# A hybrid layer's mixer: state-space constants whose second forms are exchanged halves, angles counted in turns, and the recurrent decay as an exponential

## The chip, the cores and the metric

The kernel runs on one core of a Trainium2 chip. The metric is the device time of one execution in microseconds. The core's engines work side by side, each through its own queue in order: PE (matrix products, with weight loads shown as PEld), DVE and POOL (element-wise work), ACT (functions from tables, evictions, scaled copies) and SP, which issues the DMAs. An instruction waits on semaphores for what it reads, and everything behind it on its engine waits with it.

## The reference

One layer over 2048 positions of width 1024: a mixer of three branches, then a mixture of experts. The change is in branches B and C of the mixer.

```python
z = rms_norm(h, norm_g) @ w_in                # split into A (gated MLP), B (recurrent), C (state space)

def mixer_rglru(x_raw, g_raw, ...):           # B: 384 channels
    xc = causal_depthwise_conv(x_raw, conv_w, conv_b)
    r = sigmoid(xc @ rg_w + rg_b)             # per head of 64
    i = sigmoid(xc @ ig_w + ig_b)
    log_a = -8.0 * r * softplus(-lam)
    a = exp(log_a)
    b = sqrt(-expm1(2.0 * log_a)) * (i * xc)
    h = linear_recurrence(a, b)               # h_t = a_t h_{t-1} + b_t
    return h * gelu(g_raw)

def mixer_s5(x_raw, a_re, a_im, log_dt, b_re, b_im, c_re, c_im, d, ...):   # C: 16 groups x 16 channels
    lam = a_re + 1j * a_im                    # 64 complex states in each group
    lam_bar = exp(lam * exp(log_dt))
    b_bar = (lam_bar - 1.0) / lam * (b_re + 1j * b_im)
    state = linear_recurrence(lam_bar, b_bar x)
    y = gelu((c_mat state).real + d * x)
    return y * sigmoid(y @ glu_w + glu_b)

y = concat(rms_norm(y_a), rms_norm(y_b), rms_norm(y_c)) @ w_out
h = h + y
h = h + hierarchical_moe(rms_norm(h))         # top-1 group, top-2 experts in it
return rms_norm(h, final_norm_g)
```

## The kernel before

The program has two parts. The first makes the three branches, the output projection and the routing; the second (from about 835 us) runs the experts block by block. Everything the change touches is in the first.

**How the first part is staged.** The sequence is done in two halves (h = 0, 1) of 1024 positions. For each half the columns of `w_in` come in chunks of 256: for h = 0 in the order A0, C, B0, B1, B2, A1, A2. A chunk is multiplied in full precision by three matmuls on split operands (lines 90 to 92, output `z`), the operands being a high part and a remainder of the transposed, normalised input (`xT`) and of the weights (`w`, made on ACT at lines 212 and 216 and on POOL). What belongs to a branch after its matmuls is written as a generator. A small class `Flow` advances all living generators by one step at each tick, and ticks stand between the matmuls of the chunks (after every twelve of a B chunk); a `yield n` lets n ticks pass, a `yield 0` goes on in the same tick after the others. A table `TURNS`, keyed by a generator's number and its step, overrides some of those numbers. So the program's order on each engine is fixed when it is built: constants, recurrent pieces and weight preparation are woven into the sequence of matmuls, and at run time each queue goes through that order.

**`s5_consts`** makes the constants of branch C once, on the fly, while the B chunks are multiplied. For the 16 groups it needs the powers 0 to 8 of `lam_bar` (`pw`: real and imaginary part, powers, groups), the input matrices `bb1` and `bb2` (real and imaginary rows stacked on 128 partitions, and a second form), the output matrices `tcc[0]` and `tcc[1]` in the same two forms, and tables of cosine and sine of 130 multiples of each state's angle. It goes through the groups four at a time, so in four rounds:

- `angles` (lines 661 to 687): the multiples `k * phi` of an angle that is split into a coarse part `phi` and a remainder `plo` are formed on 128 x 4 x 130 elements, reduced by multiples of 2 pi with a rounding through integers and a two-part constant, clamped, and given to the sine on ACT; the cosine is one minus twice the squared sine of the half angle. Both tables go to device memory (`cstT`), and their last columns to `cs128`.
- the loop at lines 700 to 738: `outer` multiplies powers by matrices on POOL and DVE (128 x 512 in `big`, 128 x 576 in `m1..`/`m2..`), sums and differences of the products are made on POOL, the input matrices are transposed on PE and evicted by ACT, and both forms go to device memory (`cstP`, five slots of 16 x 128 columns: 0 and 1 are the two forms of the input matrices, 3 and 4 those of the output matrices, 2 the direct kernel). The direct kernel `kp` of the four groups comes from a PE product and goes to `kpad`, from which eight DMAs (line 740) fill slot 2 after the last round.

The state-space work itself (`c_batch`, two groups at a time, eight batches per half) reads `cstP` and `cstT` back with DMAs (lines 784 to 788), so it starts after the fourth round.

**`b_post`** is the recurrent branch for one piece: 128 channels (i = 0..2) of 512 positions (q = 0, 1) of a half, so twelve pieces in all, six for each half. The convolution runs on DVE on the matmul's result (`bxc`), the two gate products on PE (line 922, bank `m`), tanh of the half argument on ACT in place of the sigmoids (line 923). Then the decay and its root (lines 926 to 941). With `sp` the softplus times two in column 0 of `b_cols` and `tr` the tanh of the gate, the second tanh (line 926) is T = tanh(-log_a / 2), the root of T is made on ACT, and on DVE 1/(1 + T), from which sqrt(1 - a^2)/2 = sqrt(T)/(1 + T) and a = 2/(1 + T) - 1. A scan on DVE makes the recurrence, POOL multiplies by the gate (`bgg`), ACT squares it (line 946) and PE sums the squares (line 950).

A function of ACT needs its table set: gelu and tanh are in one set here, the sine and the root in others, and a change of set is an instruction of its own (ACT_TABLE_LOAD), which the compiler places.

## Time and profile before

| | us |
|---|---|
| median of 3 runs (lowest to highest) | 1661.69 (1660.15 to 1671.78) |
| profiled execution, its own time | 1667.31 |
| its span | 1665.5 |
| PE busy in the span | 1510.0 (91%) |
| DVE busy | 1028.5 (62%) |
| ACT busy | 915.6 (55%) |
| POOL busy | 693.2 (42%) |

Busy shares are means over stages with different limits, so they say little about one edit. The page's second part cuts the span into 40 slices of 41.6 us and gives each engine's busy tenths and the granted clock of PE in them:

```profile
PE   7885689989999999989589969999999999999993
...
DVE  6399876367365165777888877578788767403001
ACT  6455345656755556543144635666566656656662
POOL 1286412142202153442144534556555555545442
PEclk8998799999999999999789989999999999999996
```

PE is near full in most slices; the third to fifth are the ones in which DVE stands at 8 or 9 and PE falls to 5 and 6. These are the slices of the constants and of the first four recurrent pieces. The time of a stage is read from the engine whose queue is full in it; the prediction cuts the span at 88 and 204 us, where the constants' rounds begin and end, and at 300 and 600.

### The profile page before, as it was taken

What the parts mean: (1) busy time and instruction counts of PE and PEld (TensorE: products, weight loads), DVE (VectorE), ACT (ScalarE), POOL (GpSimd) and SP (SyncE); (2) the same over time, 40 slices, a digit from 0 to 9 for tenths busy, and PEclk for the clock granted to TensorE, in tenths of its full rate; (3) what the DMA queues carried; (4) which work ended last, traced back from release to release, by engine and by line L of the source; (5) the groups of instructions that cost most, each with busy time, mean ns of one, the idle gap of its engine ahead of it and who ended that gap; (6) DMA issues with size and microseconds to landing.
All of it is one profiled execution on the core that took longest, in us unless ns stands there. A gap on an engine that the chain in (4) does not pass through costs nothing.

```text
span 1665.5 us, 25734 instructions
## 1 busy us (share of the span) xinstructions
PE 1510.0 (91%) x8389; PEld 1295.1 (78%) x8390; DVE 1028.5 (62%) x1813; ACT 915.6 (55%) x2029; POOL 693.2 (42%) x553
## 2 busy tenths in 40 slices
PE   7885689989999999989589969999999999999993
PEld 6763469966788999989578858888888888888882
DVE  6399876367365165777888877578788767403001
ACT  6455345656755556543144635666566656656662
POOL 1286412142202153442144534556555555545442
PEclk8998799999999999999789989999999999999996
DMA  6232572331262352940677878678978876633442
GB/s 165 70 71 60 95 208 78 114 102 51 77 209 64 134 202 77 339 155 37 220 256 228 247 239 243 172 196 261 280 228 244 251 223 195 176 83 96 86 115 79
DMA packets 210063, 267.47 MB, mean 161 GB/s; under 512 B 30600, under 2 KB 174160, under 8 KB 209936
## 3 DMA queue, kind: packets, MB, share of 16 engines
q1 hardware_dynamic: 185456, 203.52, 38.6%
q0 software_dynamic: 24480, 62.27, 15.5%
q8 instruction: 78, 1.28, 0.3%
q14 instruction: 49, 0.40, 0.1%
HBM read 217.09 MB, written 76.94 MB: 177 GB/s over the span
## 4 chain that ended last, share of the span: by engine, by line
PE 61%; DVE 14%; DMA 6%; ACT 3%; issue 2%; POOL 1%; SPq 1%; POOLq 0%; DVEq 0%; ACTq 0%
PE pg L1693 21%; PE z L90 6%; PE z L92 6%; PE z L91 6%; PE pd L1734 4%; PE pd L1733 4%; PE pd L1732 4%; DMA stg<-in_expert_w_up_dram 3%; DVE ring L1601 2%; DVE ring L1619 2%; PE pt L1700 2%; DVE btr L932 1%; PE pt L1705 1%; PE ph L1700 1%; PE m L246 1%
## 5 line engine op out<-in xcount | busy, mean ns | idle before, releaser
L1693 PE MATMUL pg<-ring,xs 128*128 x2016 | 488.2, 395 | 14.1 <-DVE ring L1619 13.0
L1693 PEld LDWEIGHTS pg<-ring,xs 128*128 128x128 f32 x2016 | 378.5, 190 | 94.3 <-issue 16.5
L90 PE MATMUL z<-w,xT 128*128 128x256 f32 (+1 forms) x848 | 252.3, 297 | 17.9 <-ACT xT L302 8.9
L169 POOL TENSOR_TENSOR w<-raw,w 128x512 fp32r<-128x512 f32 x84 | 115.0, 1371 | 348.3 <-ACT raw L216 302.9
L92 PE MATMUL z<-w,xT 128*128 128x256 f32 (+1 forms) x848 | 246.5, 291 | 5.8 <-DVE xT L169 5.7
L91 PE MATMUL z<-w,xT 128*128 128x256 f32 (+1 forms) x848 | 245.9, 290 | 0.0
L1601 DVE TENSOR_SCALAR ring<-stg,gcol 128x512 fp32r<-128x512 f32 x242 | 133.3, 612 | 166.4 <-PE pg L1693 86.7
L1619 DVE SCALAR_TENSOR_TENSOR ring<-stg,gcol,ring 128x512 fp32r<-128x512 f32 x248 | 218.4, 940 | 0.0
L90 PEld LDWEIGHTS z<-w,xT 128*128 128x128 f32 x848 | 166.1, 196 | 21.7 <-issue 10.4
L92 PEld LDWEIGHTS z<-w,xT 128*128 128x128 f32 x848 | 165.6, 195 | 7.2 <-DVE xT L169 7.2
L91 PEld LDWEIGHTS z<-w,xT 128*128 128x128 f32 x848 | 166.2, 196 | 1.7 <-issue 1.7
L1897 POOL DMA_INDIRECT hd<-yb,tab x41 | 75.8, 1848 | 180.5 <-ACT yb L1836 180.5
L1732 PE MATMUL pd<-ring,hh 128*128 x336 | 131.5, 391 | 1.7 <-DVE hh L1638 1.7
L1733 PE MATMUL pd<-ring,hh 128*128 x336 | 131.2, 390 | 0.0
L1734 PE MATMUL pd<-ring,hh 128*128 x336 | 131.2, 390 | 0.0
L1911 POOL TENSOR_TENSOR hs<-hs,hu 128x256 f32<-128x256 f32 x84 | 102.1, 1215 | 54.0 <-ACT hu L1815 51.5
L1946 POOL TENSOR_TENSOR yb<-yb,gf 128x1024 f32<-128x1024 f32 x40 | 117.0, 2924 | 6.8 <-ACT hu L1861 6.8
L171 DVE SCALAR_TENSOR_TENSOR ht<-z,rsd,ht 128x256 f32<-128x256 f32 x176 | 84.7, 483 | 49.8 <-PE z L92 40.3
L90 PE MATMUL z<-xT,w 128*128 128x512 f32 x256 | 113.4, 443 | 0.2 <-ACT xT L302 0.2
L212 ACT ACTIVATE w<-raw,vec 128x256 fp32r<-128x256 f32 x176 | 86.6, 495 | 48.1 <-PE z L92 47.2
L91 PE MATMUL z<-xT,w 128*128 128x512 f32 x256 | 103.6, 405 | 0.2 <-DVE xT L169 0.2
L92 PE MATMUL z<-xT,w 128*128 128x512 f32 x256 | 103.1, 403 | 0.0
(443 smaller groups left out, 2862.0 us busy)
## 6 DMA issues: line engine op xcount, KB each, us to landing
stg<-in_expert_w_gate_dram SPq DMA_DIRECT2D x62, 512.0 KB
stg<-in_expert_w_up_dram SPq DMA_DIRECT2D x62, 512.0 KB
stg<-in_expert_w_down_dram SPq DMA_DIRECT2D x60, 512.0 KB
raw<-in_w_in_dram SPq DMA_DIRECT2D x48, 256.0 KB
raw<-in_w_out_dram SPq DMA_DIRECT2D x24, 512.0 KB
ht<-in_x_dram SPq DMA_DIRECT2D x16, 512.0 KB
yp<-yTd SPq DMA_DIRECT2D x8, 1024.0 KB
hd<-ht SPq DMA_DIRECT2D x16, 512.0 KB
```

What stands on the lines that cost most here:

```text
L90: nc.tensor.matmul(ps, ah, bh, start=first, stop=False)
L91: nc.tensor.matmul(ps, ah, bl, start=False, stop=False)
L92: nc.tensor.matmul(ps, al, bh, start=False, stop=last)
L169: tt = lambda o, a, b, op, e=V: e.tensor_tensor(out=o, in0=a, in1=b, op=op)
L1601: x = v.tensor_scalar(out=ring[:, r, 0, sl], in0=src[:, sl], scalar1=g, scalar2=None, op0=OP.mult)
L1619: x = v.scalar_tensor_tensor(out=ring[:, r, 1, sl], in0=src[:, sl], scalar=g, in1=hi, op0=OP.mult, op1=OP.subtract)
L1693: i = t.matmul(pg[f], xx[j // 2], w[j % 2], start=k == 0 and j == 0, stop=k == 7 and j == 2)
L1732: t.matmul(pd[n], hh[:, 0, kf], w[0], start=kf == 0, stop=False)
L1733: t.matmul(pd[n], hh[:, 0, kf], w[1], start=False, stop=False)
L1734: i = t.matmul(pd[n], hh[:, 1, kf], w[0], start=False, stop=kf == 3)
L1911: g.tensor_tensor(out=o, in0=o, in1=hu[:, f * 256:(f + 1) * 256], op=OP.mult).then_inc(s_hm, 1)
L1946: g.tensor_tensor(out=z, in0=z, in1=gf, op=OP.mult).then_inc(p_z, 1)
```

## The change

Three things are changed.

**Second forms as exchanged halves.** The sign of `swp` and the place of the minus are arranged so that slot 1 of `cstP` is slot 0 with its two halves of 64 columns exchanged, and slot 4 is slot 3 with its two halves of 64 partitions exchanged. So in each round `outer` runs twice instead of four times on each of POOL and DVE, two POOL additions go, four of the eight transposes and one of two evictions go, and slots 1 and 4 are written by two DMAs each, from the same tiles as slots 0 and 3.

**Angles in turns.** `phi` and `plo` are kept in turns (one turn is 2 pi), and `trn` is the whole angle in turns. ACT makes `k * trn` with a column scale; adding and subtracting 12582912 rounds it to whole turns on DVE; eight fused DVE steps, one group of 128 x 130 at a time, make `k * phi - round` and add `k * plo`; the factor 2 pi is the scale of the sine, with the sign of the lower half folded into it (`sg2`). The square, the scale and shift that make the cosine, and the two copies into `cs128` are on ACT instead of POOL and DVE.

**The decay as an exponential.** Column 3 of the tile `b_cols` holds minus 4 times the softplus, and a = exp(log_a) comes straight from ACT, in place of the reciprocal. With T as before, sqrt(1 - a^2)/2 = (1 + a) sqrt(T)/2, which is one fused DVE step on `bsq` and `btr` (the root takes its argument times 0.25).

```diff
-            p8, phi, plo = sm("p8"), sm("phi"), sm("plo")
+            p8, phi, plo, trn, sg2 = sm("p8"), sm("phi"), sm("plo"), sm("trn"), sm("sg2", 1)
...
-            ts(ni, p8, 4096.0, None, OP.mult)
+            ts(trn, p8, 1.0 / TWO_PI, None, OP.mult)
+            ts(ni, trn, 4096.0, None, OP.mult)
...
-            tt(plo, p8, phi, OP.subtract)
+            stt(plo, phi, -C1, p8, OP.mult, OP.add)
+            stt(plo, phi, -C2, plo, OP.mult, OP.add)
+            ts(plo, plo, 1.0 / TWO_PI, None, OP.mult)
+            ts(sg2, sgn, TWO_PI, None, OP.mult)
...
             ts(sp, t3, 2.0, None, OP.mult)
+            ts(b_cols[:, :, 3], t3, -4.0, None, OP.mult)
...
-            V.tensor_copy(swp[0:64, 64:128], ident[0:64, 0:64])
+            ts(swp[0:64, 64:128], ident[0:64, 0:64], -1.0, None, OP.mult)
...
             def angles():
...
-                    tt(ang, bg(phi), bk, OP.mult, G)
-                    tt(an3, bg(plo), bk, OP.mult)
+                    for j in range(4):
+                        A.activation(an2[:, j], kk, AF.Copy, scale=trn[:, g + j:g + j + 1])
                     yield 2
-                    tt(an2, ang, an3, OP.add)
-                    ts(ani, an2, 1.0 / TWO_PI, None, OP.mult)
-                    V.tensor_copy(an2, ani)
-                    stt(ang, an2, -C1, ang, OP.mult, OP.add)
-                    stt(ang, an2, -C2, ang, OP.mult, OP.add)
-                    tt(ang, ang, an3, OP.add)
-                    ts(ang, ang, 3.1415925, -3.1415925, OP.min, OP.max)
+
+                    ts(an2, an2, 12582912.0, 12582912.0, OP.add, OP.subtract)
+                    for j in range(4):
+                        stt(ang[:, j], kk, phi[:, g + j:g + j + 1], an2[:, j], OP.mult, OP.subtract)
+                    for j in range(4):
+                        stt(ang[:, j], kk, plo[:, g + j:g + j + 1], ang[:, j], OP.mult, OP.add)
+                    ts(ang, ang, 0.49999997, -0.49999997, OP.min, OP.max)
                     yield
-                    A.activation(an2, ang, AF.Sin, scale=0.5)
-                    A.activation(ang, ang, AF.Sin)
-                    tt(an2, an2, an2, OP.mult, G)
+                    A.activation(an2, ang, AF.Sin, scale=TWO_PI / 2)
+                    A.activation(ang, ang, AF.Sin, scale=sg2)
+                    A.activation(an2, an2, AF.Square)
+                    A.activation(an2, an2, AF.Identity, scale=-2.0, bias=ones)
                     yield
-                    ts(an2, an2, -2.0, 1.0, OP.mult, OP.add)
-                    V.tensor_copy(cs128[:, 0, g:g + 4], an2[:, :, 129])
-                    G.tensor_copy(cs128[:, 1, g:g + 4], ang[:, :, 129])
+                    A.activation(cs128[:, 0, g:g + 4], an2[:, :, 129], AF.Copy)
+                    A.activation(cs128[:, 1, g:g + 4], ang[:, :, 129], AF.Copy)
...
-                for slot, (x, y) in enumerate(((0, 1), (1, 0))):
-                    us.append((v4(big[2 * slot]), v4(big[2 * slot + 1])))
-                    outer(G, us[slot][0], bb1, 8, x, g)
-                    outer(V, us[slot][1], bb2, 8, y, g)
+                us = v4(big[2 * i]), v4(big[2 * i + 1])
+                outer(G, us[0], bb1, 8, 0, g)
+                outer(V, us[1], bb2, 8, 1, g)
...
-                for i, op in enumerate((OP.add, OP.subtract)):
-                    tt(us[i][0], us[i][0], us[i][1], op, e=G)
-                    yield 0
-                    tt(ms[i][1], ms[i][1], ms[i][0], op, e=G)
+                tt(us[0], us[0], us[1], OP.add, e=G)
+                yield 0
+                tt(ms[1], ms[1], ms[0], OP.add, e=G)
                 yield 2
...
+                nc.sync.dma_start(out=dst(0), in_=o)
+                nc.sync.dma_start(out=dst(3), in_=m)
+                for j in range(2):
+                    here, there = slice(j * 64, j * 64 + 64), slice(64 - j * 64, 128 - j * 64)
+                    nc.sync.dma_start(out=dst(1)[:, :, here], in_=o[:, :, there])
+                    nc.sync.dma_start(out=dst(4)[here], in_=m[there])
...
-            A.activation(tr, tr, AF.Tanh, scale=b_cols[:, i, 0:1], bias=b_cols[:, i, 0:1])
+            sq = bw.tile([P, N], F32, name="bsq")
+            A.activation(sq, tr, AF.Tanh, scale=b_cols[:, i, 0:1], bias=b_cols[:, i, 0:1])
             stt(ti, ti, 1.0, xc, OP.add, OP.mult)
-            sq = bw.tile([P, N], F32, name="bsq")
-            A.activation(sq, tr, AF.Sqrt)
-            yield
-            ts(tr, tr, 1.0, None, OP.add)
-            V.reciprocal(out=tr, in_=tr)
-            yield 0
-            tt(sq, sq, tr, OP.mult)
+            A.activation(tr, tr, AF.Exp, scale=b_cols[:, i, 3:4], bias=b_cols[:, i, 3:4])
+            A.activation(sq, sq, AF.Sqrt, scale=0.25)
+            yield
+            stt(sq, tr, 1.0, sq, OP.add, OP.mult)
             yield 0
             tt(ti, ti, sq, OP.mult)
             yield 0
-            ts(tr, tr, 2.0, -1.0, OP.mult, OP.add)
             V.tensor_tensor_scan(out=xc, data0=tr, data1=ti, initial=hst[:, i, 3:4], op0=OP.mult, op1=OP.add)
```

**What stands in the queues.** Apart from these instructions the order of each engine stays as it was, but for one step in the second half of the sequence, where a piece has one `yield 0` less: the sums of squares of a late piece (line 950) stand 52 rows of PE's program earlier than before, with its product on POOL and its square on ACT a few rows from their old places. Three places follow. First ACT's queue in the first recurrent piece, from the second tanh to the next piece's convolution input (`btr`, `bsq`, `bxc`), before:

```order
L926 ACTIVATE btr<-btr,b_cols 128x512
L929 ACT_TABLE_LOAD
L929 ACTIVATE bsq<-btr 128x512
L906 ACTIVATE bxc<-z,vec 128x512
L679 ACT_TABLE_LOAD
```

And now:

```order
L929 ACTIVATE bsq<-btr,b_cols 128x512
L931 ACT_TABLE_LOAD
L931 ACTIVATE btr<-btr,b_cols 128x512
L932 ACT_TABLE_LOAD
L932 ACTIVATE bsq<-bsq 128x512
L908 ACTIVATE bxc<-z,vec 128x512
L680 ACT_TABLE_LOAD
```

A table load and the exponential stand between the tanh and the root, and the convolution input of the next piece stands behind both. Over the whole program ACT has 46 table loads where it had 34.

Right behind it on ACT stand the sines of the second round of constants (`an`, `ang`), the eviction of the transposed matrices (`big`) and the next gelu, before:

```order
L679 ACTIVATE an_1165<-ang 128x520
L680 ACTIVATE ang<-ang 128x520
L727 ACTIVATE big_338<-tp 128x512 x2
L916 ACT_TABLE_LOAD
L916 ACTIVATE bgg<-z 128x512
```

And now:

```order
L680 ACTIVATE an_1164<-ang 128x520
L681 ACTIVATE ang<-ang,sg_588 128x520
L682 ACTIVATE an_1164<-an_1164 128x520
L683 ACTIVATE an_1164<-an_1164,ones 128x520
L724 ACTIVATE big_338<-tp 128x512
L685 ACTIVATE cs_276<-an_1164 128x4
L686 ACTIVATE cs_276<-ang 128x4
L670 ACTIVATE an_1302<-kk,trn 128x130 x4
L918 ACT_TABLE_LOAD
L918 ACTIVATE bgg<-z 128x512
```

The square, the cosine's scale and shift, the copies to `cs128` and the scaled copies for the third round have come in, and one of two evictions is gone. The same round on DVE, from the last step of the round before it to the clamp, before:

```order
L170 TENSOR_SCALAR an_999<-an_999 128x520
L684 COPY cs_276<-an_999 128x4
L169 TENSOR_TENSOR an_1166<-plo,kk 128x520
L691 TENSOR_TENSOR big_338<-pw,big_337 128x512 x2
L691 TENSOR_TENSOR m_1203<-pw,big_337 128x576
L691 TENSOR_TENSOR m_1207<-pw,big_337 128x576
L169 TENSOR_TENSOR an_1165<-ang,an_1166 128x520
L170 TENSOR_SCALAR an_1165<-an_1165 128x520
L673 CAST an_1165<-an_1165 128x520
L171 SCALAR_TENSOR_TENSOR ang<-an_1165,ang 128x520 x2
L169 TENSOR_TENSOR ang<-ang,an_1166 128x520
L170 TENSOR_SCALAR ang<-ang 128x520
```

And now:

```order
L692 TENSOR_TENSOR big_338<-pw,big_337 128x512
L692 TENSOR_TENSOR m_1201<-pw,big_337 128x576
L170 TENSOR_SCALAR an_1164<-an_1164 128x520
L171 SCALAR_TENSOR_TENSOR ang<-kk,phi,an_1164 128x130 x4
L171 SCALAR_TENSOR_TENSOR ang<-kk,plo,ang 128x130 x4
L170 TENSOR_SCALAR ang<-ang 128x520
```

Fourteen instructions have become twelve, eight of which are a quarter as long; the rest of DVE's round, the recurrent piece between these and the next round, has lost the reciprocal and two scale-and-shift steps.

29 lines of the change are left out of this document (11 added, 18 removed).

## The prediction

> **What bounds the kernel now.** I read the page's span first, then busy time by stage, then TensorE's waits in the stage that the change touches, then ScalarE's.
>
> ```profile
> span 1665.5 us, 25734 instructions
> ```
>
> Busy microseconds of PE, its weight loads, DVE, ACT and POOL in three stretches, with counts, then PE's granted clock, the DMA share and GB/s:
>
> ```profile
> core 0: us, PE busy (x) PEld busy (x) DVE busy (x) ACT busy (x) POOL busy (x), PEclk, DMA share, GB/s
> 88.00:204.00 116.00, 75.55 (x310) 53.64 (x309) 113.34 (x127) 56.87 (x91) 79.65 (x62) 0.83 0.36 75
> 204.00:300.00 96.00, 87.11 (x550) 74.59 (x549) 62.23 (x136) 47.40 (x96) 16.08 (x21) 0.95 0.50 139
> 300.00:600.00 300.00, 285.81 (x1816) 252.04 (x1815) 146.53 (x281) 185.04 (x426) 67.09 (x53) 0.96 0.38 122
> ```
>
> The whole change lies in these three stretches: the constants of the state-space branch are made between 88 and 204 us, and the twelve recurrent pieces run in all three. In the first stretch DVE is busy 113.34 of 116 us, PE only 75.55, at a granted clock of 0.83. PE is idle for 116 - 75.55 = 40.4 us there, but for 8.9 us in the next 96 and 14.2 us in the 300 after. So only 88 to 204 has much to give. What ends PE's waits there (total, times, longest):
>
> ```profile
> PE m L922 <- DVE kp L735: 20.3, 3, 7.0
> PE m L922 <- DVE bxc L171: 11.4, 3, 4.6
> PE tp L725 <- POOL big L169: 8.5, 4, 2.7
> ```
>
> These three make 40.2 of the 40.4 us, and 31.7 of them wait on DVE directly. ScalarE (ACT) waits in the same stretch:
>
> ```profile
> ACT an L679 <- DVE ang L170: 31.0, 4, 8.7
> ACT bxc L946 <- POOL bgg L169: 20.8, 3, 8.2
> ```
>
> ACT is idle for 116 - 56.87 = 59.1 us. 31.0 are the sine waiting for DVE's last step on the angles. 20.8 are the square of the gated product, which waits for POOL, which waits for the DVE scan. 7.3 are left for everything else. DVE's queue is the bound of this stretch, and PE and ACT follow it.
>
> **The change, part by part. DVE in the stretch.** The products in `outer` are halved on both engines. They take, DVE first, then POOL:
>
> ```profile
> 88.00:204.00 116.00, 23.46 (x16) 25.16 (x16) 0.83 0.36 75
> ```
>
> Half of 23.46 is 11.7 us off DVE, and half of 25.16 is 12.6 off POOL. The other DVE rows of the stretch that the change touches (total, then mean ns):
>
> ```profile
> L171 DVE SCALAR_TENSOR_TENSOR ang<-an,ang 128x520 f32<-128x520 f32 x8 | 10.6, 1320 | 0.3
> L932 DVE RECIPROCAL btr<-btr 128x512 f32<-128x512 f32 x3 | 10.1, 3353 | 0.1
> ...
> L171 DVE SCALAR_TENSOR_TENSOR bxc<-hst,vec,bxc 128x3 f32<-128x3 f32 (+2 forms) x12 | 6.4, 532 | 0.0
> ...
> L170 DVE TENSOR_SCALAR an<-an 128x520 int32<-128x520 f32 (+1 forms) x8 | 7.5, 938 | 0.1
> L169 DVE TENSOR_TENSOR an<-ang,an 128x520 f32<-128x520 f32 x4 | 7.1, 1773 | 0.0
> ...
> L673 DVE CAST an<-an 128x520 f32<-128x520 int32 x4 | 5.7, 1436 | 0.1
> L169 DVE TENSOR_TENSOR ang<-ang,an 128x520 f32<-128x520 f32 x4 | 4.7, 1182 | 0.1
> L684 DVE COPY cs<-an 128x4 f32<-128x4 f32 x4 | 4.3, 1066 | 0.1
> ...
> L170 DVE TENSOR_SCALAR btr<-btr 128x512 f32<-128x512 f32 x6 | 3.8, 632 | 0.0
> ...
> L170 DVE TENSOR_SCALAR ang<-ang 128x520 f32<-128x520 f32 x4 | 2.8, 701 | 0.1
> L169 DVE TENSOR_TENSOR an<-plo,kk 128x520 f32<-128x520 f32 x4 | 2.8, 688 | 0.0
> ```
>
> Removed for the angles: 10.6 + 7.5 + 7.1 + 5.7 + 4.7 + 4.3 + 2.8 + 2.8 = 45.5 us. Removed in three recurrent pieces: the reciprocal's 10.1 and two scale-and-shift steps, 3.8, so 13.9; the product with `sq` becomes one fused step of about the same cost. Added for each of four groups: one rounding step at the 938 ns of the `an` row, one clamp at the 701 ns of the `ang` row, and eight fused steps on 128x130. The trace has no such shape. It lies between the same operation on 1 to 3 columns (532 ns here with POOL in its way) and on 520 columns (1320); since 130 is nearest to the small end, and the small one has mostly waiting in it, I take 500, with 250 and 750 as ends. That is 4 x (0.94 + 0.70 + 4.0) = 22.6 us, ends 14.6 and 30.6. DVE then needs 113.3 - 11.7 - 45.5 - 13.9 + 22.6 = 64.8 us. The extra column constants (a second step on `b_cols`, three small steps on `plo`, one on `sg2`) are some 0.2 us each ahead of or at the start of the stretch, 1 us at most.
>
> **ACT in the stretch.**
>
> ```profile
> L212 ACT ACTIVATE w<-raw,vec 128x256 fp32r<-128x256 f32 x18 | 8.9, 495 | 0.0
> ...
> L727 ACT ACTIVATE big<-tp 128x512 f32<-128x512 f32 x8 | 4.3, 582 | 0.0
> L929 ACT ACT_TABLE_LOAD x3 | 3.8, 1283 | 0.1
> L906 ACT ACTIVATE bxc<-z,vec 128x512 f32<-128x512 f32 x4 | 3.1, 771 | 2.6 <-PE m L950 1.4 <-PE z L92 1.1
> ...
> L680 ACT ACTIVATE ang<-ang 128x520 f32<-128x520 f32 x4 | 2.5, 637 | 0.1
> L926 ACT ACTIVATE btr<-btr,b_cols 128x512 f32<-128x512 f32 x3 | 2.4, 803 | 0.0
> ```
>
> ```profile
> L514 ACT ACTIVATE s<-ph 128x16 f32<-128x16 f32 x1 | 0.2, 215 | 0.0
> ```
>
> For each group ACT gains four scaled copies of 128x130 (between 0.22 for 16 columns and 0.50 for 256 with a column scale; 0.40 taken), a square of 520 columns (0.64), a scale-and-shift of 520 (0.77, as the row of L906), two copies of four columns (0.22 each) and a column scale in the sine (0.80 of L926 against 0.64, so 0.16). It loses one eviction (0.58). That is 1.60 + 0.64 + 0.77 + 0.44 + 0.16 - 0.58 = 3.0 us, four times 12.1. For each recurrent piece it gains an exponential (0.80, scale and bias are columns, like L926) and a table load (1.28): 2.1 us, three in the stretch 6.3. The order shows 46 table loads where there were 34, so none of the twelve merges with another. ACT then needs 56.9 + 12.1 + 6.3 = 75.3 us. So ACT, not DVE, would carry the most work, with PE beside it: 75.55 less the sixteen transposes that go, and its work shrinks if the clock rises above 0.83.
>
> **The sum for the stretch.** If ACT never waited, the stretch would take 75.3 and the gain would be 40.7 us. If it kept the 7.3 us of waits that are not behind DVE's angles or the scan, 82.6. I add 3 us for the first group, in which the products and the angles still run one after another on DVE before ACT has a sine to do: 85.6, a gain of 30. The work that hides ACT's own 18 us is gone then; what is late next is the square behind POOL and the weight preparation, both in ACT's own order. POOL falls from 79.65 by half of its products, half of the additions that follow them and the steps on angles, so it does not bound.
>
> **A rule weighed here.** In the second piece the hyperbolic tangent, the load and the square root stand on ACT so (start, us):
>
> ```profile
> 145.41 0.80 ACT L926 ACTIVATE btr<-btr,b_cols 128x512 f32<-128x512 f32 x1
> 146.22 1.28 ACT L929 ACT_TABLE_LOAD   x1
> 147.52 0.64 ACT L929 ACTIVATE bsq<-btr 128x512 f32<-128x512 f32 x1
> ```
>
> From the start of the tangent to the start of the root are 2.11 us, which is 0.80 and 1.28 and almost nothing between. The Trainium skill ("ScalarE: Activation LUTs", What ACT_TABLE_LOAD costs) says that each switch costs 1283 ns for the load and about 1380 ns for a drain, 2.66 us in all, and advises batching by table set; this change does the opposite. By that page the three loads in the stretch would cost 4.1 us more, and the sum would be 26 instead of 30. The trace agrees on the load and shows no drain, so my sum uses 1.28.
>
> **DMA and SP.** Four of the 256 KB writes to `cstP` (slot 1) are split into two halves of 64 columns and four (slot 4) into halves of 64 partitions, so SP issues 9 instead of 7 in a group. At the end of the stretch SP shows:
>
> ```profile
> 202.80 0.32 SPq L737 DMA_DIRECT2D kpad<-kp  x1
> ...
> 204.75 7.69 SPq L740 DMA_DIRECT2D cstP<-kpad  x8
> ```
>
> The last group's write of `kp` starts at 202.80 and the eight reads of it occupy SP for 7.69 us until 212. The new halves are issued ahead of that write, when the eviction is done, and are read only after those eight. They cost two issues a group (0.4 us each, of which only the last group's can show: 0.8 us), and are otherwise covered by those 7.7 us; if that cover went, up to 3 us of a landing would show. I count 0, ends 0 and 3.
>
> **After the stretch.** The reciprocal by itself, in the two later stretches, shows where the other nine pieces run (DVE busy, count):
>
> ```profile
> 204.00:300.00 96.00, 10.06 (x3) 0.95 0.50 139
> 300.00:600.00 300.00, 20.12 (x6) 0.96 0.38 122
> ```
>
> From 204 to 300 three pieces run beside a PE that is 91% busy; I count 1 us (ends -2 and +4). From 300 to 600 PE's waits that end with a recurrent piece are these:
>
> ```profile
> PE m L922 <- DVE bxc L171: 3.4, 2, 2.1
> PE tp L239 <- ACT btr L923: 2.1, 1, 2.1
> PE m L997 <- ACT btr L923: 1.7, 1, 1.7
> PE m L950 <- ACT btr L923: 0.7, 1, 0.7
> ```
>
> They add up to 7.9 us. Each of the six pieces there gets 3.35 + 2 x 0.42 shorter on DVE and 2.1 longer on ACT, in its own chain and in front of what queues behind it on ACT (evictions, the next convolution's input). So about half goes: 4 us, ends -4 (six pieces at 2.1 on a full ACT, less 8) and +8. The one matmul that moves (the sums of squares of a late piece stand one piece of work earlier) I count at 0; its cover is that ACT makes the squares about as much earlier.
>
> **Sum.** 30 + 1 + 4 = 35 us off the profiled execution's 1667.3 us gives 1632. That execution is 5.6 us above the median of the three runs, so against the median of 1661.7 I predict 1627 us.
>
> **Rivals.**
> (a) DVE's queue only gets shorter by what POOL's share of it lets go, and hand-offs take the place of work: the sine still waits for the clamp in each group, and the square for POOL. If half of the 51.8 us of those two waits stays, the stretch takes 75.3 + 7.3 + 25.9 = 108.5, a gain of 8, and with 2 from later the median is 1652. For it: in ACT's order the sine of a group stands right behind the root of a piece, and that behind its exponential, so one late step holds them all. Against it: DVE falls to 65 of 116, so the clamp should stand ready.
> (b) The stretch goes to the bound. ACT waits for nothing (40.7) and the clock and later pieces give all of 9: 50 us, 1612. For it: PE, DVE and ACT all have less than 76 us to do. Against: three queues that hand work to each other in order never all fit.
> (c) Slower: ACT becomes the bound at once, because its waits are hand-offs and not lateness of DVE. The place is the same stretch; the price is 18.4 us there, and with all 59.1 us of idle time kept the stretch takes 134 and the median is 1680. It decides as soon as ACT's idle time falls by less than 18.4 us. Against it: 31.0 us of that idle time end with one DVE row, in front of which 45.5 us of DVE work go.
> (d) The halves in memory are what matters: slot 1 is now written in runs of 256 bytes. The reads behind it wait, and the 7.7 us of cover are used up. The price is 3 us, or at a landing twice as long as the eight reads some 8: gain 27, 1635. The Trainium skill ("DMA: Bandwidth & Descriptors", Specifications) asks for at least 512 bytes for full rate and says that smaller writes are read, changed and written back; no run here shows the rate of a 256-byte write. Within my range.
>
> **How the numbers follow.** The forecast with (d) inside it has a chance of 0.72: gains of 18 to 45 us. (a) has 0.15, of which 0.06 lie above the 16.6 us that are 1%; (b) beyond 45 us 0.08; (c) and other losses 0.05, of which 0.03 beyond 1%. A change of 1% is about what a measurement of this kernel tells from none. So faster by over 1%: 0.72 + 0.08 + 0.06 = 0.86; within 1%: 0.11; slower: 0.03. The range that leaves out 2 in 10 goes from (b)'s 1610 to 1648, inside (a).
>
> **What would show it.** Right: DVE in the stretch of the constants under 70 us and not full; the wait of the sine on the clamp down from 31.0 to a few us; TensorE's wait on `kp` down from 20.3; the last `kp` landing near 172 instead of 203; 46 table loads of 1283 ns with no gap behind them; clock above 0.83. Wrong: fused steps on 128x130 at 750 ns or more, ACT idle for over 30 us of the shorter stretch, or PE waiting later for evictions that stand behind an exponential. A result above 1648 would mean that hand-offs, not DVE's amount of work, set the pace.

## The result and the profile after

| | us |
|---|---|
| kernel before, median of 4 runs beside it (lowest to highest) | 1662.65 (1660.15 to 1671.78) |
| changed kernel, median of 4 runs (lowest to highest) | 1612.70 (1610.21 to 1613.94) |
| ratio, 95% interval | 0.9688, 0.9649 to 0.9727 |
| profiled execution of the changed kernel, its own time | 1610.21 |

The change makes the kernel 50 us faster. 35 us were forecast. The time lies in the forecast range, near its lower end.

The span is 1608.4 us. Three stretches that answer to the three of the prediction (same columns). The first of them starts 2 us later than before, as this profile was that much behind from the start, and ends where the constants end, at 162 us instead of 203:

```profile
90.00:162.00 72.00, 64.98 (x294) 48.17 (x293) 66.64 (x111) 68.82 (x120) 37.68 (x33) 1.00 0.60 116
162.00:258.00 96.00, 86.72 (x563) 75.28 (x562) 52.13 (x128) 56.60 (x106) 16.80 (x21) 0.96 0.51 146
258.00:555.00 297.00, 285.69 (x1836) 253.10 (x1835) 119.48 (x271) 200.29 (x444) 68.67 (x55) 0.97 0.39 126
```

The stretch of the constants went from 116 to 72 us. DVE is busy 66.64 us in it and no longer alone: ACT has 68.82, PE 64.98 at a granted clock of 1.00 instead of 0.83. TensorE's largest wait there, then ScalarE's (total, times, longest):

```profile
PE m L924 <- DVE kp L737: 4.2, 3, 2.5
```

```profile
ACT bxc L908 <- PE z L92: 1.1, 1, 1.1
```

PE's idle time fell from 40.4 to 72 - 64.98 = 7.0 us, ACT's from 59.1 to 3.2: the sine's 31.0 us behind the clamp and the square's 20.8 behind POOL are both gone. DVE's rows in the stretch (total, mean ns, idle before):

```profile
L170 DVE TENSOR_SCALAR an<-an 128x520 f32<-128x520 f32 x4 | 13.0, 3256 | 2.5 <-ACT an L670 2.5
L171 DVE SCALAR_TENSOR_TENSOR ang<-kk,plo,ang 128x130 f32<-128x130 f32 x16 | 11.3, 770 | 0.0
L171 DVE SCALAR_TENSOR_TENSOR ang<-kk,phi,an 128x130 f32<-128x130 f32 x16 | 4.6, 350 | 0.1
...
L170 DVE TENSOR_SCALAR ang<-ang 128x520 f32<-128x520 f32 x4 | 3.7, 919 | 0.1
...
L692 DVE TENSOR_TENSOR m<-pw,big 128x576 f32<-128x576 f32 x4 | 3.0, 744 | 0.0
...
L692 DVE TENSOR_TENSOR big<-pw,big 128x512 f32<-128x512 f32 x4 | 2.7, 676 | 0.0
```

The angles cost 13.0 + 11.3 + 4.6 + 3.7 = 32.6 us, and the products 5.7. The products are not only half as many, each is also half as long as before. The rounding step takes 3.3 us on average, which nothing in the trace of before suggested; the last section comes back to it.

After the stretch one wait of PE is longer than before (3.4 us at this place then). Its largest from 162 to 200 us, and two slices of 6 us:

```profile
PE tp L751 <- DMA big<-in_a_spatial_w_dram: 6.5, 2, 6.1
```

```profile
168.00:174.00 6.00, 0.94 (x5) 0.41 (x3) 0.00 (x0) 4.53 (x6) 0.00 (x0) 1.00 0.83 184
174.00:180.00 6.00, 3.80 (x15) 3.06 (x16) 4.50 (x10) 3.04 (x6) 1.28 (x1) 0.52 1.01 297
```

The row names the load of the spatial weights. SyncE issues it at 172.18 us, right behind the eight reads of the constants' round trip through memory. Transfers fill 83 to 101% of the queues' time beside this wait, and PE works at a granted clock of 0.52 right after it.

### The profile page after: what moved, and what is told of

Its sections match the earlier page's. It is cut to its first block, busy times and chain, and to the rows that moved or that the text cites. A ratio compares the mean times of both kernels' runs of the same rounds, so it can differ in the third digit from the quotient of the medians.

```text
span 1608.4 us, 25675 instructions
## 1 busy us (share of the span) xinstructions
PE 1496.2 (93%) x8373; PEld 1290.0 (80%) x8374; DVE 935.0 (58%) x1774; ACT 948.7 (59%) x2081; POOL 653.3 (41%) x525
## 3 DMA queue, kind: packets, MB, share of 16 engines
q8 instruction: 78, 1.28, 0.3%
## 4 chain that ended last, share of the span: by engine, by line
PE 68%; DVE 14%; ACT 6%; DMA 6%; issue 2%; SPq 1%; POOL 1%; POOLq 0%; DVEq 0%; ACTq 0%
PE pg L1692 23%; PE z L90 7%; PE z L92 7%; PE z L91 7%; PE pd L1733 4%; PE pd L1731 4%; PE pd L1732 4%; DMA stg<-in_expert_w_up_dram 3%; DVE ring L1618 2%; DVE ring L1600 2%; PE pt L1699 2%; DMA xp<-in_x_dram 1%; PE pt L1704 1%; PE ph L1699 1%; DVE bxc L171 1%
## 5 line engine op out<-in xcount | busy, mean ns | idle before, releaser
L1618 DVE SCALAR_TENSOR_TENSOR ring<-stg,gcol,ring 128x512 fp32r<-128x512 f32 x248 | 209.6, 906 | 0.0
L1910 POOL TENSOR_TENSOR hs<-hs,hu 128x256 f32<-128x256 f32 x84 | 101.0, 1202 | 52.2 <-ACT hu L1814 51.3
L90 PE MATMUL z<-xT,w 128*128 128x512 f32 x256 | 110.2, 431 | 0.2 <-ACT xT L302 0.2
L91 PE MATMUL z<-xT,w 128*128 128x512 f32 x256 | 102.0, 399 | 0.2 <-DVE xT L169 0.2
L92 PE MATMUL z<-xT,w 128*128 128x512 f32 x256 | 101.5, 397 | 0.0
```

The source lines that it names most:

```text
L90: nc.tensor.matmul(ps, ah, bh, start=first, stop=False)
L91: nc.tensor.matmul(ps, ah, bl, start=False, stop=False)
L92: nc.tensor.matmul(ps, al, bh, start=False, stop=last)
L1618: x = v.scalar_tensor_tensor(out=ring[:, r, 1, sl], in0=src[:, sl], scalar=g, in1=hi, op0=OP.mult, op1=OP.subtract)
L1910: g.tensor_tensor(out=o, in0=o, in1=hu[:, f * 256:(f + 1) * 256], op=OP.mult).then_inc(s_hm, 1)
```

## The experiments

Beside the times stand three lengths from the profiles. All are counted from one mark ahead of the stretch, the start of PE's transposes on line 298 that begin at 58.66 us in the profile of before, because profiles of kernels that are alike up to there differ by up to 3.7 us at it. They run to the start of SyncE's last write of `kp` (the end of the constants), to the second batch of state-space products on PE, and to the twelfth scan on DVE. "Gain" is against the median of the kernel before on the same chip.

| kernel | median us | ratio (95% interval) | gain | mark | to last `kp` write | to second batch | to twelfth scan |
|---|---|---|---|---|---|---|---|
| before | 1662.65 |  |  | 58.66 | 144.14 | 165.6 | 478.1 |
| changed | 1612.70 | 0.9688 (0.9649 to 0.9727) | 50.0 | 60.65 | 101.13 | 122.8 | 423.6 |
| halves alone | 1640.43 | 0.9863 (0.9834 to 0.9893) | 24.1 | 57.66 | 124.98 | 148.3 | 457.4 |
| turns alone | 1649.55 | 0.9905 (0.9873 to 0.9937) | 14.9 | 58.49 | 131.05 | 153.1 | 468.2 |
| decay alone | 1647.08 | 0.9888 (0.9850 to 0.9927) | 17.4 | 60.94 | 131.55 | 156.0 | 458.7 |
| without the turns | 1628.76 | 0.9789 (0.9748 to 0.9829) | 33.8 | 60.40 | 112.68 | 138.2 | 441.2 |
| halves' writes cut again | 1620.14 | 0.9738 (0.9709 to 0.9766) | 44.4 | 60.07 | 103.93 | 128.1 | 430.6 |
| less on ScalarE, more on GpSimd | 1617.82 | 0.9724 (0.9682 to 0.9767) | 44.7 | 57.28 | 105.71 | 130.5 | 433.3 |
| 5.4 us of ScalarE left out | 1585.66 | 0.9546 (0.9519 to 0.9573) | 73.9 | 59.02 | 97.33 | 119.5 | 421.7 |
| 11.3 us of VectorE left out | 1611.65 | 0.9704 (0.9676 to 0.9732) | 47.9 | 58.51 | 100.99 | 125.1 | 428.0 |
| rounding with two operands | 1609.97 | 0.9675 (0.9635 to 0.9714) | 52.6 | 60.09 | 101.47 | 123.3 | 424.4 |
| loads early, two queues | 1611.79 | 0.9694 (0.9651 to 0.9738) | 50.7 | 58.92 | 101.12 | 125.8 | 428.2 |
| reads early | 1615.32 | 0.9724 (0.9700 to 0.9749) | 44.3 | 58.85 | 107.11 | 130.7 | 433.2 |
| cosine's end on VectorE | 1622.53 | 0.9749 (0.9724 to 0.9774) | 42.1 | 58.96 | 108.88 | 132.8 | 435.1 |

### Each part alone: halves

The kernel before, with the loop of the changed kernel and the sign in the sine:

```diff
-                    A.activation(ang, ang, AF.Sin)
+                    A.activation(ang, ang, AF.Sin, scale=sgn)
```

> The kernel before with the exchanged halves alone: one loop's products, the half transfers, and the sign moved into the sine; old angles and old decay. Theory 1 (the stretch of the constants is bound by the amount of VectorE's work, so each part is worth the VectorE time that it takes out): 4 products of 1668 ns and 4 of 1382 ns go, 12.2 us; if the 8 that stay also fall to what the profile after shows (744 and 676 ns), 6.4 us more. Gain 12 to 19 us, all of it before 204 us, nothing later. Theory 2 (most of the gain of the whole change comes from GpSimd working less beside VectorE, and this part halves GpSimd's products): gain 25 us or more, and VectorE's untouched operations in the stretch get shorter too. If the hand-offs between engines bound the stretch and not the work: under 8 us.

Gain 24.1 us; 144.14 - 124.98 = 19.2 of it by the last `kp` write. The stretch, and DVE's products in it:

```profile
90.00:183.00 93.00, 67.73 (x277) 48.58 (x276) 90.89 (x110) 51.88 (x81) 52.00 (x43) 0.86 0.48 93
```

```profile
L691 DVE TENSOR_TENSOR big<-pw,big 128x512 f32<-128x512 f32 x4 | 5.6, 1398 | 0.0
L691 DVE TENSOR_TENSOR m<-pw,big 128x576 f32<-128x576 f32 x4 | 5.0, 1262 | 0.0
```

DVE is still full, 90.89 of 93 us, so its work still sets the pace. The products went from 23.7 to 10.6 us, 13.1 less. The other 6 us of the gain in the stretch are about what DVE operations that were not touched lost in length, beside a POOL with half its products (the eight fused steps on 520 columns fell from 10.6 to 8.5 us, the integer conversion from 5.7 to 3.7). So both theories have a part: about two thirds is work removed, and one third, as I read it, is less company from POOL.

### Each part alone: turns

The angles of the changed kernel in the kernel before; the sine's scale carries no sign:

```diff
-                    A.activation(ang, ang, AF.Sin, scale=sg2)
+                    A.activation(ang, ang, AF.Sin, scale=TWO_PI)
```

> The kernel before with the angles in turns alone (four steps of ScalarE, rounding by adding and subtracting a large number, fused steps with a scalar of each partition, square and 1-2x on ScalarE); all four products of each kind, the old decay. Theory 1: VectorE's angle work falls from 45.5 us to the 32.6 us of the profile after, or to 21 us if the rounding step doesn't wait beside GpSimd: gain 13 to 24 us, all before 204 us. Here GpSimd has twice the products, so if GpSimd is what held the rounding step, its mean (3256 ns after) is no shorter and the gain is nearer 13. Theory 2 (contention of GpSimd's products): under 10 us, since they stay.

Gain 14.9 us, within the expected span. Stretch and DVE rows:

```profile
90.00:190.00 100.00, 71.84 (x300) 51.77 (x298) 96.70 (x117) 63.85 (x116) 63.84 (x48) 0.86 0.44 87
```

```profile
L171 DVE SCALAR_TENSOR_TENSOR ang<-kk,plo,ang 128x130 f32<-128x130 f32 x16 | 17.2, 1133 | 0.0
L171 DVE SCALAR_TENSOR_TENSOR ang<-kk,phi,an 128x130 f32<-128x130 f32 x16 | 16.5, 1091 | 0.1
```

DVE is full again (96.70 of 100). What I expected of the single rows was wrong: the rounding step took 0.72 us here and not 3.3, while the fused steps took 1.1 us and not 0.35 to 0.77. The sixteen products, of which none was removed, fell from 23.7 to 15.2 us (the first of them starts at 89.26 us, ahead of the window). The time that DVE loses beside POOL moves to whatever DVE does at that moment; it is not a property of one row.

### Each part alone: decay

The changed recurrent piece and column 3 of `b_cols` alone, in the kernel before:

```diff
+            ts(b_cols[:, :, 3], t3, -4.0, None, OP.mult)
...
-            V.reciprocal(out=tr, in_=tr)
...
+            A.activation(tr, tr, AF.Exp, scale=b_cols[:, i, 3:4], bias=b_cols[:, i, 3:4])
+            A.activation(sq, sq, AF.Sqrt, scale=0.25)
...
+            stt(sq, tr, 1.0, sq, OP.add, OP.mult)
```

> The kernel before with the decay as an exponential alone. Theory 1: in the stretch 3 reciprocals (10.1 us), 6 one-operand steps (3.8 us) and 3 products (2.1 us) go and 3 fused steps (2.0 us) come: 14 us less on VectorE, gain 14 us before 204 us; then the 6 us that the change as a whole wins between 204 and 430 us and keeps: together 18 to 21 us. If the later 6 us belong to another part, 14 us alone. If the extra table load and exponential on ScalarE (2.1 us each, three in the stretch) eat the gain: under 8 us.

Gain 17.4 us: 12.6 by the last `kp` write, 19.4 by the twelfth scan. So this part also wins time behind the stretch, and in it DVE stays full:

```profile
90.00:193.00 103.00, 77.33 (x312) 54.80 (x311) 100.68 (x121) 62.77 (x97) 78.94 (x62) 0.85 0.42 84
```

By the last `kp` write the three parts win 19.2 + 13.1 + 12.6 = 44.9 us alone and 43.0 together. They add up, as amounts of work on one full queue do. By the medians of whole runs they win 56.4 us alone and 50.0 together, which the intervals don't tell apart.

### Two parts together, and the turns taken out

The changed kernel with the angles of before, and the sign of the exchanged halves in the sine:

```diff
-                    A.activation(ang, ang, AF.Sin, scale=sg2)
+                    A.activation(ang, ang, AF.Sin, scale=sgn)
```

> The changed kernel with its angles put back as before (exchanged halves and new decay stay). If the three parts are each worth the VectorE work they remove and simply add, this gives the sum of the two parts alone, 24.1 and 17.4: a gain of 41 us over the kernel before. Theory of the floor (in the changed kernel ScalarE, not VectorE, ends the stretch): VectorE gets the old angles at the lengths of the run with the halves alone, 40.6 us in place of 32.6, so 75 us in place of 67, and ScalarE loses 13 of its 69; VectorE is the bound again at 98 per cent, the stretch is 76 to 78 us in place of 72, gain 43 to 46 us. If the turns were only ever a burden once ScalarE is full: no slower than the changed kernel, gain 50.

Gain 33.8 us, less than each of the numbers expected.

```profile
90.00:173.00 83.00, 68.61 (x292) 49.96 (x293) 80.83 (x108) 59.99 (x91) 52.86 (x46) 0.92 0.54 104
```

DVE is full again, and the last `kp` write comes 112.7 us after the mark instead of 101.1. That is a gain of 31.5 in the stretch, the sum of halves and decay alone (19.2 + 12.6 = 31.8). So the turns are worth nearly as much on top of the others (11.6 us) as alone (13.1). The VectorE work of 75 us that I had expected was too little, mostly since I had left the products at 5.7 us: with the old angles they take 1393 and 1264 ns each again, 10.7 us.

### The halves' writes

Each half transfer is cut in two once more:

```diff
-                for j in range(2):
-                    here, there = slice(j * 64, j * 64 + 64), slice(64 - j * 64, 128 - j * 64)
+                for j in range(4):
+                    k = (j + 2) % 4
+                    here, there = slice(j * 32, j * 32 + 32), slice(k * 32, k * 32 + 32)
```

> The changed kernel with its half transfers cut in two again: slot 1 is written in runs of 32 columns (128 bytes) and slot 4 in runs of 32 partitions, four transfers each and not two. If the short writes cost nothing on the path (transfers lie under the angles and the next group's products): the time of the changed kernel within 2 us, gain over the kernel before 48 to 52 us. If the halves cost 3 to 8 us as the prediction's rival has it, doubling them costs as much again: gain 42 to 47 us, with the wait on the transfers after the last group longer by it.

Gain 44.4, 5.6 us less than the changed kernel's; the ratios are 0.9738 and 0.9688, and their intervals overlap. The end of the stretch, VectorE's last step on `kp` and SyncE's rows around it, in the changed kernel and then in this one:

```profile
161.10 0.62 DVE L169 TENSOR_TENSOR kp<-kp,dg 16x64 f32<-16x64 f32 x1
160.92 0.59 SPq L730 DMA_DIRECT2D cstP<-m  x1
161.78 0.37 SPq L739 DMA_DIRECT2D kpad<-kp  x1
...
166.94 5.14 SPq L742 DMA_DIRECT2D cstP<-kpad  x8
```

```profile
160.53 0.62 DVE L169 TENSOR_TENSOR kp<-kp,dg 16x64 f32<-16x64 f32 x1
162.62 1.28 SPq L731 DMA_DIRECT2D cstP<-m  x1
164.00 0.36 SPq L740 DMA_DIRECT2D kpad<-kp  x1
```

VectorE has `kp` ready 101.1 us after the mark in both. In the changed kernel SyncE's last half issue is over by then (161.51 us, against 161.72 for `kp`), so the write waits for VectorE. With four more issues SyncE is busy until 163.90 and the write comes 2.8 us later, some 0.7 us for each. So the two issues that the change itself added to the last group cost nothing ahead of this write; they just fit beside VectorE's work, with 0.2 us left. That the gain falls between the 42 and 47 us of the second theory does not show that the first halves cost as much.

From the mark the second batch comes 5.4 us later. Of these the 2.6 us behind the write are no more than the round trip varies by without any such edit: from the last `kp` write to the second batch it takes 21.5 us in the kernel before, 21.6 in the changed kernel, 21.9 with the rounding in another form and 24.8 in the next experiment; the last three have the same transfers. Whether the short runs cost anything beside their issues stays open.

### Less work on ScalarE, moved to GpSimd

```diff
-                    for j in range(4):
-                        A.activation(an2[:, j], kk, AF.Copy, scale=trn[:, g + j:g + j + 1])
+                    tt(an2, trn[:, g:g + 4].unsqueeze(2).to_broadcast((P, 4, 130)),
+                       kk.unsqueeze(1).to_broadcast((P, 4, 130)), OP.mult, G)
...
-                    A.activation(an2, an2, AF.Square)
+                    tt(an2, an2, an2, OP.mult, G)
...
+                    G.tensor_copy(cs128[:, 0, g:g + 4], an2[:, :, 129])
+                    G.tensor_copy(cs128[:, 1, g:g + 4], ang[:, :, 129])
```

> The changed kernel with 10 us less on ScalarE in the stretch: the four steps that multiply the column numbers by the turns are one product on GpSimd, the square of the half sine and the cosine's and sine's last columns go back to GpSimd. If ScalarE is what bounds the stretch now (69 us busy in 72): the stretch shortens to what VectorE (67 us) and TensorE (65) allow, 68 to 69 us, and the gain over the kernel before is 53 to 54 us. If VectorE and TensorE stand as close as ScalarE and GpSimd's 9 us more lengthen VectorE's operations: no gain or 1 to 5 us lost against the changed kernel, gain 45 to 50.

No gain: the stretch is 4.6 us longer than the changed kernel's. ScalarE's waits in it:

```profile
ACT bxc L945 <- POOL bgg L169: 5.0, 2, 3.6
ACT an L680 <- DVE ang L170: 4.0, 2, 3.0
ACT an L683 <- POOL an L169: 1.6, 4, 0.4
```

The wait of the gated product's square for POOL and the sine's for DVE, which had gone with the change, come back, with a new one on POOL; together 10.6 us, as much as the work that was taken away. GpSimd's own work rose too (49.83 us in the stretch, 37.68 in the changed kernel's), and VectorE's fused steps beside it took 26.2 us for 15.9. So this did not tell whether ScalarE's work is the bound, and it does not part the hand-offs from GpSimd's added work.

### ScalarE's or VectorE's work left out

Two kernels take work away and put none in its place:

```diff
-                    A.activation(an2, an2, AF.Square)
-                    A.activation(an2, an2, AF.Identity, scale=-2.0, bias=ones)
```

> The changed kernel without the square and the 1-2x of the cosine (8 ScalarE steps, 2.5 + 2.9 us), with nothing put in their place; the cosine table holds the half sine, so that part of the computation is left out. If ScalarE's work is what ends the stretch of the changed kernel (98 per cent busy from 100 to 160 us): the last group's rows are written 4 to 5 us earlier, at 156.5 to 158 us in place of 161.7, and the gain over the kernel before grows from 50 to about 54. If no one engine does (the earlier run with ScalarE relieved got no shorter, but gave GpSimd and VectorE more): under 2 us.

```diff
-                    for j in range(4):
-                        stt(ang[:, j], kk, plo[:, g + j:g + j + 1], ang[:, j], OP.mult, OP.add)
```

> The changed kernel without the 16 fused steps of the angle's low part (11.3 us of VectorE); that part of the computation is left out, so the angles are coarser. If ScalarE's work ends the stretch: under 1.5 us earlier than 161.7 us, no more gain. If VectorE still does, with its 67 us of 72 as they stand: 8 to 11 us earlier, at 151 to 154 us. If the two pass the bound between them group by group: 3 to 6 us.

5.4 us less on ScalarE made the way from the mark to the last `kp` write 3.8 us shorter (97.3 for 101.1); 11.3 us less on VectorE made it 0.1 us shorter (101.0). Counted to VectorE's last step on `kp`, behind which the write waited for SyncE's queue in the second kernel, the second number is 1.0 us (100.05 for 101.07). Where VectorE's time went without its 16 steps (window from 90 to 161 us, then its largest wait):

```profile
90.00:161.00 71.00, 65.60 (x293) 48.42 (x291) 52.13 (x85) 68.47 (x118) 38.10 (x32) 1.00 0.63 122
```

```profile
DVE bxc L171 <- ACT bxc L906: 10.1, 3, 5.8
```

VectorE does 14.5 us less and waits 10.1 us for ScalarE's convolution input instead. So ScalarE's work ends the stretch of the changed kernel, as the prediction had it; 3.8 of 5.4 us is the share that the next bounds left. The run with less VectorE work is no faster than the changed kernel in its median either (47.9 against 50.0).

The 1585.66 us of the first of the two is not a gain of the stretch: by the twelfth scan it is 2 us ahead. The rest lies among the experts, and goes with its other output: TensorE's gate and up products there, of the changed kernel and then of this one:

```profile
L1692 PE MATMUL pg<-ring,xs 128*128 x2016 | 488.0, 395 | 8.6 <-DVE ring L1618 7.3 <-issue 1.2
```

```profile
L1690 PE MATMUL pg<-ring,xs 128*128 x1920 | 468.1, 397 | 21.3 <-DVE ring L1616 20.5 <-issue 0.7
```

96 of the 2016 products are not there. Times of kernels whose output differs can be compared only ahead of what depends on the data.

### The rounding step in another form

```diff
-                    ts(an2, an2, 12582912.0, 12582912.0, OP.add, OP.subtract)
+                    stt(an2, an2, 12582912.0, rbig.unsqueeze(2).to_broadcast((P, 4, 130)), OP.add, OP.subtract)
```

> The changed kernel with the rounding step in a form with two tensor operands (the large number subtracted comes from a column broadcast), which computes the same. In the changed kernel two of the four steps took 5.43 and 6.76 us while GpSimd worked without a gap, the other two 0.42. If a one-operand step waits until GpSimd pauses and a two-operand step takes turns with it: all four take 0.6 to 1.5 us and VectorE's work falls by 8 to 10 us. If any VectorE operation waits so: the mean stays at 3 us. On the time: with ScalarE as the bound, 0 to 3 us gained against the changed kernel (50 to 53 over the kernel before); with VectorE as the bound, 8.

The time is that of the changed kernel within what the runs can tell (52.6 against 50.0, 0.9675 and 0.9688), which fits a stretch bound by ScalarE. The expectation on the row fell: VectorE is busy 66.64 us in its 71 as it was in 72, since the wait moved to the neighbours (the last section).

### The round trip after the constants

First the order: the spatial weights are loaded after the third group, and the eight reads are dealt to two queues.

```diff
-                nc.sync.dma_start(out=cstP[s * 16:(s + 1) * 16, 2, :, :], in_=...
+                (nc.gpsimd if s % 2 else nc.sync).dma_start(out=cstP[s * 16:(s + 1) * 16, 2, :, :], in_=...
```

> The changed kernel with the round trip after the constants shortened: the two loads of the spatial weights are issued after the third group, whose buffers are free by then, and the eight reads of the convolution's padded rows are dealt to SyncE's queue and GpSimd's in turn (5.1 us of issues on one queue before). If the order of issues on SyncE's queue sets TensorE's idle time of 8 us between 160 and 180 us: the reads that the first batch needs start 3 to 4 us earlier and the wait shrinks by as much, gain over the kernel before 53 to 54 us. If the transfers' own time sets it: under 1 us against the changed kernel. If the extra queue delays what GpSimd issues: slower.

50.7 us, no different from the changed kernel. The first batch starts 2.2 us earlier after the mark (115.2 for 117.3), the second 3.0 later. The wait only moved: TensorE no longer waits for the weights' load, but 3.4 us for VectorE's copy of the weights and 3.2 us for the first batch's read of `cstT`.

Then the bytes:

```diff
             for g in range(0, 16, 4):
+                if g == 12:
+                    rows8(0, 12)
...
-            for s in range(8):
-                nc.sync.dma_start(out=cstP[s * 16:(s + 1) * 16, 2, :, :], in_=kpad[:, :, s:s + 8, :].rearrange("c g t e -> c g (t e)"))
+            rows8(12, 16)
```

> The changed kernel with the end of its round trip emptied: the eight reads of the convolution's padded rows are done for the first twelve column groups while the last group is computed, so that after it only a quarter of their bytes is left, and the spatial weights are loaded after the third group. The wait of TensorE (8 us without work between 160 and 180 us, then a granted clock of 0.5 for 6 us) stood beside transfers at 83 to 101 per cent of the queues' time, and dealing the reads to two queues didn't shorten it. If the bytes set it: the first batch starts 3 to 6 us earlier and the kernel is 4 to 8 us faster than the changed one, gain 54 to 58. If the count of transfers or a landing's own delay sets it: within 2 us of the changed kernel; if eight more reads hold up SyncE's queue inside the stretch: slower by up to 5.

The gain is 44.3 us, 5.7 less than the changed kernel's, with intervals of the ratios that overlap. By the profile, which shows the longest of its four executions (1621.90 us), the second batch comes 7.9 us later after the mark. SyncE's queue at the end of the stretch:

```profile
152.64 7.68 SPq L703 DMA_DIRECT2D cstP<-kpad  x8
...
162.01 0.44 SPq L731 DMA_DIRECT2D cstP<-big  x1
...
169.62 5.39 SPq L703 DMA_DIRECT2D cstP<-kpad  x8
```

The early reads hold the queue from 152.64 to 160.32, and the last group's writes, which began at 158.15 in the changed kernel, begin at 162.01. VectorE has `kp` ready 101.1 us after the mark, as in the changed kernel; the write comes 6.0 us behind it. The late reads have a quarter of the bytes and still take 5.39 us to issue. The round trip behind the last write is no shorter with fewer bytes either (130.7 - 107.1 = 23.6 us; 21.6 in the changed kernel). So the third theory of the expectation holds, issues that hold up SyncE's queue inside the stretch; neither form of the round trip that was tried is better than the changed kernel's.

### The cosine's end on VectorE

```diff
-                    A.activation(an2, an2, AF.Square)
-                    A.activation(an2, an2, AF.Identity, scale=-2.0, bias=ones)
                     yield
+                    stt(an2, an2, -2.0, an2, OP.mult, OP.mult)
+                    ts(an2, an2, 1.0, None, OP.add)
```

> The changed kernel with the cosine's last two steps (square, 1-2x: 5.4 us of ScalarE in all) on VectorE, as a fused step and a one-operand step, about 0.7 and 0.5 us each for four groups, 4.7 us of VectorE. Nothing is left out. Leaving those two steps out moved the last group's rows 3.6 to 5.4 us earlier, and taking 11.3 us from VectorE 1.4 us. If ScalarE's work is the bound and VectorE's 5 us of room hold the two steps: 2 to 4 us faster than the changed kernel, gain over the kernel before 52 to 54 us. If the hand-off back from ScalarE to VectorE takes it away, as it did where GpSimd got the work (5 us slower): gain 45 to 49, with a wait of VectorE on ScalarE's sine of 2 us or more and fused steps of over 1 us.

The gain is 42.1 us, 7.9 less than the changed kernel's and below both expected spans. The last `kp` write comes 7.8 us later after the mark, although ScalarE has 5.4 us less to do and the two steps cost VectorE little (0.68 and 0.43 to 1.41 us). The largest wait of ScalarE and of VectorE in its stretch, from 88 to 168 us:

```profile
ACT cs L685 <- DVE an L170: 14.2, 4, 5.0
```

```profile
DVE bxc L171 <- ACT bxc L908: 8.4, 3, 4.9
```

ScalarE's next step, the copy of four cosines, now waits 14.2 us for VectorE, and what stands behind it in ScalarE's order holds up VectorE (8.4 us) and TensorE (7.9 us behind `btr`) in turn. Here a hand-off in the middle of a full queue cost more than twice the 5.4 us of work that it took away. The place of the wait was not the one expected (VectorE on the sine).

## Why the prediction came out

**The bound: right.** VectorE was 97 to 98% busy in every kernel that lacked a part of the change, and the three parts add up at the end of the stretch.

**VectorE's new amount: right by errors that cancel, so by luck.** 64.8 us were predicted, 66.6 measured. The fused steps took 15.9 us (16 counted), though the two kinds took 770 and 350 ns and not 500 each. The rounding step took 13.0 for 3.8 (I had priced it at the mean of two forms in one row, 1397 and 478 ns), the clamp 3.7 for 2.8. Against that the remaining products took 5.7 us for 11.7, because I halved their number and not their length, and untouched steps got shorter too (those on 1 to 3 columns 4.2 for 6.4).

**ScalarE next: right in kind, its waits mis-sized.** Most of what lies between 35 and 50 us was lost here: the stretch was put at 75.3 of work + 7.3 of waits + 3 of start = 85.6 us, a gain of 30, and came out at 72, a gain of 43, with 68.8 us of ScalarE's work. The prices of single instructions were right (copies 0.39 for 0.40, square 0.62 for 0.64, exponential 0.82 for 0.80). The work was 6.5 us less for three reasons that the rows show: the first copies ran from 88.8 us, in a gap ahead of the stretch; a recurrent piece's last square and the tangent behind it slid past its end (162.41 to 163.60 us); and neighbours on ScalarE overlap, so that 13 copies of 393 ns are 4.2 us and not 5.1:

```profile
L670 ACT ACTIVATE an<-kk,trn 128x130 f32<-128x130 f32 x13 | 4.2, 393 | 0.0
```

The waits were not 7.3 but 3.2 with all idle time counted: I had carried over the waits of a queue that starves into one that is full. The 3 us for the first group's start did not show either. Rival (b), the stretch at its bound, is the case that came. The prediction gave it 0.08, and 0.72 to gains of 18 to 45 us; the time lies in the range because the range reached down to (b)'s 1610.

**The hand-offs of rival (a) did not stay.** Both links are still there in the changed kernel: the sine reads what VectorE's clamp made, and the square reads POOL's gated product. In the kernels with one part of the change, in which VectorE was still full, ScalarE waited at them: 15.0 and 21.7 us with the halves alone, 26.9 and 8.2 with the decay alone, and with the turns alone

```profile
ACT an L678 <- DVE ang L170: 18.4, 4, 6.2
ACT bxc L945 <- POOL bgg L169: 12.8, 3, 5.7
```

although there the cosine's steps stood on ScalarE already. In the changed kernel, where VectorE is no longer full, both are gone. So these waits were VectorE's lateness, as the prediction argued against (a) and (c), and not the price of the links. When a step behind the sine was put back on another engine, waits came back (10.6 and 14.2 us), one time together with more work on GpSimd.

**Table loads: right.** The same tangent, loads and root as in the prediction (start, us):

```profile
129.49 0.80 ACT L929 ACTIVATE bsq<-btr,b_cols 128x512 f32<-128x512 f32 x1
130.31 1.28 ACT L931 ACT_TABLE_LOAD   x1
131.60 0.82 ACT L931 ACTIVATE btr<-btr,b_cols 128x512 f32<-128x512 f32 x1
132.42 1.28 ACT L932 ACT_TABLE_LOAD   x1
133.72 0.63 ACT L932 ACTIVATE bsq<-bsq 128x512 f32<-128x512 f32 x1
```

Nothing stands between the rows but 0.02 us at most. The Trainium skill ("ScalarE: Activation LUTs", What ACT_TABLE_LOAD costs) adds a drain of about 1380 ns to each switch; the trace agrees on the 1283 ns of the load and shows no drain in these rows, so the extra load costs this queue 1.28 us.

**The halves' transfers: counted at 0, and nothing shows in the changed kernel.** The write of the last `kp` waits for VectorE there and not for the halves' issues, and the round trip behind it is as long as before (21.6 us for 21.5). The cover was only in part where I had put it. The 0.8 us of issues that the prediction let show for the last group were hidden ahead of the write, by VectorE's own work on `kp`; with 0.2 us left of it, four more issues showed with 2.8 us. Of rival (d) one link is visible: SyncE's eight reads begin 5.2 us behind the start of the `kp` write, for 2.0 before. But they then take 5.14 us for 7.69, so its 3 to 8 us did not come.

**After the stretch: 5 us counted, 7 left by the medians.** The stretch won 43 us by the profiles, which leaves 7 of the medians' 50. But the two profiled executions lie 57.1 us apart (1667.31 and 1610.21), and in them more falls behind the stretch: from the last `kp` write to the twelfth scan the changed kernel wins 11.4 us (333.9 us before, 322.5 after); the decay alone shows 6.8 us of that, halves alone 1.5, turns alone -3.2. So most of it comes with the decay, in the recurrent pieces. How much of it is their shorter chain, and how much a round trip or a granted clock that differs between profiles, was not separated.

## What to carry to other kernels

Where one engine's queue is full, price an edit by the work that it takes out of that queue, and expect such parts to add up until the next queue is full; then take the next queue's work as the time, without the waits that it had while it starved. Moving work off the engine that is full failed in both tries here, in which the chain had to come back to it: a whole chain on one engine was worth more than a shorter queue. What a VectorE operation takes beside GpSimd is not a property of that operation, so shortening GpSimd's work counts for VectorE as well.

## What the runs showed of the hardware

In two of the four rounds of the changed kernel VectorE was held for as long as GpSimd worked without a pause, over several GpSimd instructions, not one. A rounding step that takes 0.42 us in the other two rounds took 5.43 and 6.76; VectorE's row of the first, then the first and the last of GpSimd's four that read data (start, us):

```profile
107.92 5.43 DVE L170 TENSOR_SCALAR an<-an 128x520 f32<-128x520 f32 x1 [1.31 <-ACT an L670]
```

```profile
108.13 1.09 POOL L692 TENSOR_TENSOR big<-pw,big 128x512 f32<-128x512 f32 x1
...
111.63 1.43 POOL L169 TENSOR_TENSOR m<-m,m 128x576 f32<-128x576 f32 x1
```

The step ends at 113.35, when these four operations, which follow each other without a pause, are over. In the kernel with the two-operand rounding, GpSimd's same four operations ran from 107.81 to 113.04, and VectorE's rows there are:

```profile
107.38 0.70 DVE L171 SCALAR_TENSOR_TENSOR an<-an,rbig 128x520 f32<-128x520 f32 x1 [1.08 <-ACT an L672]
108.11 5.08 DVE L171 SCALAR_TENSOR_TENSOR ang<-kk,phi,an 128x130 f32<-128x130 f32 x4
...
144.17 7.01 DVE L171 SCALAR_TENSOR_TENSOR an<-an,rbig 128x520 f32<-128x520 f32 x1 [1.22 <-ACT an L672]
```

There the rounding came just ahead of GpSimd's chain and took 0.70 us, and the next four steps paid 5.08; another time the two-operand form itself took 7.01. So it is not the form of the operation. The Trainium skill ("SBUF — State Buffer", SBUF: two separate sides) says that GpSimd and VectorE, the latter in a two-port mode or with two inputs in SBUF, take a shared port pair as an exclusive lock for a whole instruction, and that the other one blocks. The trace agrees that one of them stands still; it adds that the one that stands still can lose the next four rounds too. That it is this lock was not tested by itself.

After 6 us in which TensorE was busy for 0.94, its granted clock fell from 1.00 to 0.52 for the next 6. The kernel before shows the same at this place: 2.40 us busy from 210 to 216 us at 1.00, then 0.51 in the next 6. If the gap is the cause, the idle time in the round trip costs more than its own length; no run here tests that.
